# A hybrid decoder block on one core: the input loaded a second time by tokens, its mean squares from row sums on ScalarE, the constants later, and two early output tiles in other PSUM banks

## The chip, the core and the metric

One core of one Trainium2 chip. The metric is the device time of one execution, in microseconds (us), of the kernel as a whole; lower is better. TensorE (PE in the profile) multiplies matrices into PSUM, VectorE (DVE), ScalarE (ACT) and GpSimd (POOL) work element by element, and SyncE (SP) issues the transfers from and to the chip's memory.

## What is computed

One layer of a hybrid block over 1024 tokens of width 1024, all in float32:

```
h = x
proj  = rms_norm(h, norm_mix_g) @ w_in            # 1536 conv columns, 1824 RWKV columns
y     = concat(short_gated_conv(proj[:, :1536]), rwkv7_time_mix(proj[:, 1536:]))
h     = h + y @ w_out
h     = h + square(relu(rms_norm(h, norm_mlp_g) @ w_up)) @ w_down
h     = h + sigmoid(rms_norm(h, norm_ple_g) @ w_ple_gate) * (p @ w_ple_proj)
out   = rms_norm(h, norm_final_g)
rms_norm(h, g) = h * rsqrt(mean(h*h, last axis) + 1e-6) * g
```

The change concerns the first `rms_norm`: the mean of the squares of each token's 1024 input values, and what waits for it.

## The kernel before

**Layout.** The input is held transposed: width on the 128 partitions (8 tiles, called d), tokens along the row, in two halves of 512 tokens (h0, h1). A tile is 128x512. Each product is made of three matmuls so as to keep float32 precision: an operand is split into a high part (`ah`, `wih`, rounded) and the residual (`al`, `wil`), and high x high, low x high and high x low are summed in PSUM.

**The start.** `start()` writes the order of the transfers on SP: the 16 tiles of x with the weights of the first two jobs among them, then the other weights. `load_x` (L434) brings a tile to one of four `tmp` buffers or to one of seven that are still unused (`r`, `k`, `vv`). `split_x` (L443) makes from it `ah` on ScalarE (scaled by the gain) and `al` on VectorE; then it squares the tile on ScalarE and, from the second tile on, adds the square to a running sum in `BK` on GpSimd (L458). A `tmp` buffer is free again when that addition has been done. When the 8 tiles of a half are in, `row_scale` (L465) sums over the partitions with matmuls against a column of ones (L263), takes mean and epsilon (L266, VectorE) and the power -1/2 (L269, GpSimd), spreads the four columns to 128x512 (L272, `tmc`), transposes them on TensorE (L276) and copies the result to `rbc` (L487): the inverse root of each token on all partitions. The norm is thus applied behind the product: each product tile is multiplied by `rbc` when it leaves PSUM (L616).

**The products.** `products()` runs through the jobs, a job being 128 columns of `w_in` (or of `w_out` later), two PSUM tiles (h0 and h1) and 48 matmuls. The first group holds two jobs (96 matmuls), both LoRA inputs; the second is the remaining 32 LoRA columns (32 matmuls, high and residual of the weights side by side in one tile, `wih`); then come r, k and v of the first head pair and so on, with the convolution's jobs in between. I count them as group 0, 1, 2, ... The output tiles come from a ring of three banks, `pmm0` to `pmm2`; only the second job of group 0 takes its two from the four `px` banks, which else serve the recurrence. A bank is free when `shifted` (L590 on) has multiplied its tile by `rbc`. `shifted` runs in the order of the jobs, on ScalarE and VectorE: for each half the product with `rbc`, the token shift, for the 32 columns first the sum of the two halves of the tile (L613), and behind the LoRA inputs tanh and a split.

**The recurrence.** For each of four head pairs and two halves there is a chain of 8 steps (`chain`). A step is three links, each a pair or one of small matmuls into the one bank `pch` and a small instruction on ScalarE or VectorE that reads it: L1044, L1045, then `pe` on ScalarE; L1053, then `uv` on ScalarE; L1065, L1066, then the state `sv` on VectorE (L1072). The matmuls of the jobs are meant to run between the links.

**Order.** All of it is written by strands to a list scheduler (`_Flow`) while the program is built: each strand names an engine, a cost and what it depends on, and the strand that could start first goes next. On the chip each engine runs its instructions in the order so written. A change of a cost or a buffer in one place moves instructions in others.

Of the kernel before, what the change touches and what calls it, by code (L numbers as in the profile page):

```python
# [14 lines left out]
ALU = mybir.AluOpType  # L15
# [197 lines left out]
def block_kernel(ctx: ExitStack, tc: tile.TileContext, a: dict, out: bass.AP):  # L213
# [101 lines left out]
    with tc.manual_schedule():  # L315
# [67 lines left out]
        def flat(t):  # L383
            return t.rearrange("p c t -> p (c t)")
# [58 lines left out]
        def split_x(h, d, xt, rel, hd):  # L443
# [5 lines left out]
            sl = ss[:, h * HT:(h + 1) * HT]  # L449
            ss_n[h] += 1  # L450
            if ss_n[h] == 1:
                e = yield "act", 620, [e]
                nc.scalar.activation(out=sl, in_=xt, func=AF.Square)
            else:
                e = yield "act", 620, [e]
                nc.scalar.activation(out=xt, in_=xt, func=AF.Square)
                e = yield "pool", 1330, [e]
                nc.gpsimd.tensor_tensor(out=sl, in0=sl, in1=xt, op=ALU.add)  # L458
            rel(e)
            ss_n[2 + h] += 1  # L460
            if ss_n[2 + h] == ND:
                fl.spawn(row_scale(h, e))

        def row_scale(h, e):

            ps, dep, rel = yield from fl.take(px, [e])
            e = yield "pe", 750, [e, dep]
            sums_of_squares(ps, ss[:, h * HT:(h + 1) * HT])
            ss_n[4] += 1
            if ss_n[4] == 2:  # L470
                ss_rel(e)
            r = small[:, 4 + 4 * h:8 + 4 * h]
            e = yield "dve", 157, [e]
            mean_plus_eps(r, ps[:, 0:4])
            rel(e)
# [17 lines left out]
        ss, _, ss_rel = BKs()  # L493
        ss = flat(ss)
        ss_n = [0] * 5
# [35 lines left out]
        def start():  # L531
            for g in range(2):
                for h in range(2):
                    for d in range(4):
                        if h == 0 and d < 2:
                            yield from load_w(d, P, g)
                        yield from load_x(h, 4 * g + d)
                if g == 0:
                    e = yield "sp", 700, []
                    nc.sync.dma_start(out=kc, in_=a["cst"])  # L540
                    kc_ready(e)
                    e = yield "sp", 200, []
                    nc.sync.dma_start(out=ident, in_=a["idn"])
                    id_ready(e)
# [6 lines left out]
        def products():  # L551
# [17 lines left out]
            for k, grp in enumerate(groups):  # L569
                out = isinstance(grp[0][0], tuple)  # L570
                halves = grp[0][2]
                for i, (ci, n, _) in enumerate(grp):
                    key = ("o", ci[0]) if out else ci
                    for h in halves:
                        tiles.setdefault(key, {})[h] = pmm() if i == 0 else (yield from fl.take(px))
# [1494 lines left out]
```

## Time and profile before

| | us |
|---|---|
| runs (3) | 1384.71, 1386.5, 1389.36; median 1386.5 |
| the profiled execution's own time | 1384.89 |
| its span in the trace | 1383.0 |
| TensorE busy | 1338.8 (97%) |
| VectorE busy | 918.5 (66%) |
| ScalarE busy | 641.7 (46%) |
| GpSimd busy | 208.0 (15%) |
| granted TensorE clock, mean | 0.984 |

The busy share is over stages with different limits. The trace times each instruction and says for idle time of an engine what ended it. A matmul that is followed at once by the next shows its whole duration, which overlaps the next one's; the pace is the difference of their starts. The granted clock is 1.00 at 2.4 GHz and 0.50 at 1.2 GHz.

### The profile page before, as it was taken

Reading aid. Unit: us, or ns where it says so; the run is one execution under the profiler, and the core shown is the slowest. Engines: PE = TensorE matmul, PEld = TensorE weight load, DVE = VectorE, ACT = ScalarE, POOL = GpSimd, SP = SyncE. Lnnn points to the kernel's source line nnn. Section 1 sums busy time; section 2 is a strip of 40 time slices with the busy share of each in tenths; the row PEclk is TensorE's granted clock in tenths of the full one; section 3 lists DMA queues with packets and bytes.
Section 4 is the critical chain, followed back from the end, with each engine's and each line's share of the span. In section 5 each row is a group of like instructions: output and inputs, shape, how many; then the busy total and the mean of one; then the engine's idle time right before and its main releaser. Section 6 shows DMA issues by size and latency. Waiting matters only on the chain.

```text
span 1383.0 us, 22259 instructions
## 1 busy us (share of the span) xinstructions
PE 1338.8 (97%) x8456; PEld 1097.6 (79%) x8456; DVE 918.5 (66%) x1484; ACT 641.7 (46%) x1210; POOL 208.0 (15%) x409
## 2 busy tenths in 40 slices
PE   8899899999999999998999999999999999999997
PEld 5687688888878787877788888888888888888886
DVE  7756666766866844548876666666556777895455
ACT  6533255354454455434654445545444444654432
POOL 8115314324224320221000000000000000000000
PEclk9999899999999998999999999999999999999999
DMA  5111012111111132653344444435797433443123
GB/s 174 51 59 41 22 28 56 45 29 41 53 36 41 60 113 89 215 183 138 122 165 152 148 160 161 142 116 189 266 352 245 142 108 96 148 133 125 55 69 91
DMA packets 107451, 161.15 MB, mean 117 GB/s; under 512 B 27376, under 2 KB 36848, under 8 KB 107344
## 3 DMA queue, kind: packets, MB, share of 16 engines
q1 hardware_dynamic: 106672, 159.43, 35.8%
q8 instruction: 66, 1.08, 0.3%
q10 hardware_dynamic: 672, 0.30, 0.1%
q14 instruction: 41, 0.34, 0.1%
HBM read 113.56 MB, written 46.14 MB: 115 GB/s over the span
## 4 chain that ended last, share of the span: by engine, by line
PE 88%; DVE 6%; issue 2%; POOL 2%; DMA 1%; ACT 1%; SPq 0%; POOLq 0%; DVEq 0%; ACTq 0%
PE px L1380 23%; PE pmm L563 23%; PE pmm L1380 18%; PE pch L1380 5%; PE px L1943 2%; PE px L1945 2%; PE px L1944 2%; PE px L819 1%; PE pch L1045 1%; PE pch L1066 1%; PE pch L1053 1%; PE pch L1044 1%; PE pch L1065 1%; DVE wil L431 1%; DVE BK L778 1%
## 5 line engine op out<-in xcount | busy, mean ns | idle before, releaser
L563 PE MATMUL pmm<-ah,wih 128*128 128x512 f32 (+1 forms) x544 | 221.9, 409 | 8.2 <-DVE pz L613 4.5
L563 PE MATMUL pmm<-al,wih 128*128 128x512 f32 (+1 forms) x544 | 222.3, 409 | 1.1 <-DVE al L447 1.1
L563 PE MATMUL pmm<-ah,wil 128*128 128x512 f32 x528 | 217.2, 411 | 4.3 <-DVE wil L431 4.3
L1300 ACT CAST ah<-big 128x512 fp32r<-128x512 f32 x176 | 108.5, 621 | 175.9 <-issue 69.5
L1295 DVE TENSOR_TENSOR al<-big,ah 128x512 fp32r<-128x512 f32 x176 | 120.1, 689 | 66.3 <-ACT ah L1300 66.1
L563 PEld LDWEIGHTS pmm<-ah,wih 128*128 128x128 f32 (+1 forms) x544 | 103.4, 190 | 28.6 <-DVE pz L613 4.9
L563 PEld LDWEIGHTS pmm<-al,wih 128*128 128x128 f32 (+1 forms) x544 | 102.8, 189 | 21.7 <-DVE al L447 2.4
L563 PEld LDWEIGHTS pmm<-ah,wil 128*128 128x128 f32 x528 | 101.1, 192 | 22.7 <-DVE wil L431 6.0
L1380 PE MATMUL px<-ah,al 128*128 128x512 f32 x264 | 102.8, 390 | 0.0
L1380 PE MATMUL px<-al,ah 128*128 128x512 f32 x264 | 102.7, 389 | 0.0
L269 POOL TENSOR_TENSOR r<-r,small 128x4 f32<-128x4 f32 x2 | 2.9, 1453 | 663.4 <-DVE r L266 663.4
L1380 PE MATMUL px<-ah 128*128 128x512 f32 x224 | 87.3, 390 | 0.0
L429 ACT CAST wih<-wir 128x512 fp32r<-128x512 f32 (+1 forms) x78 | 47.5, 609 | 83.4 <-PE pmm L563 78.7
L1295 DVE TENSOR_TENSOR al<-A,ah 128x512 fp32r<-128x512 f32 x108 | 73.3, 687 | 18.3 <-ACT ah L1300 18.0
L1380 PE MATMUL pmm<-ah,al 128*128 128x512 f32 x208 | 81.0, 389 | 0.0
L1380 PE MATMUL pmm<-al,ah 128*128 128x512 f32 x208 | 80.9, 389 | 0.0
L1300 ACT CAST ah<-A 128x512 fp32r<-128x512 f32 x108 | 66.7, 618 | 27.0 <-PE pmm L1380 23.3
L431 DVE TENSOR_TENSOR wil<-wir,wih 128x512 fp32r<-128x512 f32 x76 | 57.5, 759 | 31.5 <-ACT wih L429 31.1
L1380 PE MATMUL pmm<-ah 128*128 128x512 f32 x192 | 74.7, 389 | 0.0
L1380 PEld LDWEIGHTS px<-ah,al 128*128 128x128 f32 x264 | 49.6, 188 | 10.5
L1380 PEld LDWEIGHTS px<-al,ah 128*128 128x128 f32 x264 | 49.6, 188 | 10.5
L1072 DVE SCALAR_TENSOR_TENSOR sv<-sv,dct,pch 128x64 f32<-128x64 f32 x60 | 16.8, 279 | 60.3 <-PE pch L1066 60.0
(377 smaller groups left out, 3095.8 us busy)
## 6 DMA issues: line engine op xcount, KB each, us to landing
bd<-h SPq DMA_DIRECT2D x112, 256.0 KB, 2.3
big<-bd SPq DMA_DIRECT2D x112, 256.0 KB, 2.8
big<-in_w_up_dram SPq DMA_DIRECT2D x32, 512.0 KB, 4.1
A<-in_w_down_dram SPq DMA_DIRECT2D x64, 256.0 KB, 4.6
wir<-in_w_in_dram SPq DMA_DIRECT2D x52, 256.0 KB, 2.7
wir<-in_w_out_dram SPq DMA_DIRECT2D x24, 256.0 KB, 3.1
MB<-in_xT_dram SPq DMA_DIRECT2D x16, 256.0 KB, 3.0
hd<-h SPq DMA_DIRECT2D x16, 256.0 KB, 2.1
```

Source lines behind the costliest of these rows:

```text
L429: nc.scalar.copy(ht[:, :, 0:n], rt[:, :, 0:n])
L431: nc.vector.tensor_tensor(out=lt[:, :, 0:n] if n == P else ht[:, :, n:2 * n], in0=rt[:, :, 0:n], in1=ht[:, :, 0:n].bitcast(F32), op=ALU.su ...
L563: nc.tensor.matmul(ps[0:m], wt[:, d, 0:m], xt[:, x, :], start=first and i == 0, stop=end and i == len(ways) - 1)
L778: nc.vector.tensor_tensor(out=BK[q, :, (1 - h) * C:(2 - h) * C], in0=c3(kh)[q], in1=ei[q], op=ALU.mult)
L819: nc.tensor.matmul(g[h][4][:, c, :], BK[hs[h], c0 + c, :], LA[hs[h], c0 + c, 0:3:2, h * C:(h + 1) * C], start=True, stop=True)
L1072: nc.vector.scalar_tensor_tensor(out=nxt, in0=sv[:, c, :], scalar=dct[:, c:c + 1], in1=ps, op0=ALU.mult, op1=ALU.add)
L1295: nc.vector.tensor_tensor(out=out, in0=x, in1=y, op=ALU.subtract)
L1300: nc.scalar.copy(hi, raw)
L1380: nc.tensor.matmul(ps, wt, xt, start=start and i == 0, stop=stop and i == 2, skip_group_check=on)
L1943: nc.tensor.matmul(pg[:, c], r["hi"][:, d, o:o + P], wh[:, c], start=d == 0, stop=False)
L1944: nc.tensor.matmul(pg[:, c], r["lo"][:, d, o:o + P], wh[:, c], start=False, stop=False)
L1945: nc.tensor.matmul(pg[:, c], r["hi"][:, d, o:o + P], wl[:, c], start=False, stop=d == ND - 1)
```

## The change

- The squares, the running sum on GpSimd and the matmuls against ones go out of the first norm. A tile of x is free when `al` has been made.
- `load_tokens()` loads x once more, now as it lies in memory, 128 tokens on the partitions and their 1024 values along the row (512 KB a tile, 8 tiles), into three buffers that are unused so early: the two `MB` and `BK`. Its strand starts behind the 16 tiles of x. From the fourth tile on a load waits for the square of the third tile before it.
- `square_tokens()` squares a tile on ScalarE with `accum_out`, so the row sum falls out as a column of `small`. After four of them `row_scale` goes on as before, from the mean.
- The constants `kc` and the identity are loaded behind the first three token tiles, where they stood between the 8th and the 9th tile of x.
- In `products()`, the h1 tile of group 1 and of group 3 comes from the `px` banks.

```diff
             x_ready[h][d](e)
-            sl = ss[:, h * HT:(h + 1) * HT]
-            ss_n[h] += 1
-            if ss_n[h] == 1:
-                e = yield "act", 620, [e]
-                nc.scalar.activation(out=sl, in_=xt, func=AF.Square)
-            else:
-                e = yield "act", 620, [e]
-                nc.scalar.activation(out=xt, in_=xt, func=AF.Square)
-                e = yield "pool", 1330, [e]
-                nc.gpsimd.tensor_tensor(out=sl, in0=sl, in1=xt, op=ALU.add)
             rel(e)
...
-        def row_scale(h, e):
-
-            ps, dep, rel = yield from fl.take(px, [e])
-            e = yield "pe", 750, [e, dep]
-            sums_of_squares(ps, ss[:, h * HT:(h + 1) * HT])
...
+        def load_tokens():
+
+            places = [g() for g in (MBs, MBs, BKs)]
+            for i in range(NT):
+                t, dep, rel = places[i] if i < 3 else (places[i % 3][0], squared_x[i - 3], None)
+                e = yield "sp", 1500, [dep]
+                nc.sync.dma_start(out=flat(t), in_=a["x"][i * P:(i + 1) * P, :])
+                fl.spawn(square_tokens(i, flat(t), e, places[i % 3][2] if i + 3 >= NT else None))
+
+        def square_tokens(i, t, e, rel):
+            e = yield "act", 1250, [e]
+            nc.scalar.activation(out=t, in_=t, func=AF.Square, accum_out=small[:, 4 + i:5 + i])
+            squared_x[i](e)
+            if rel is not None:
+                rel(e)
+            if i % 4 == 3:
+                fl.spawn(row_scale(i // 4, [*squared_x[i - 3:i], e]))
+
+        def row_scale(h, deps):
+
             r = small[:, 4 + 4 * h:8 + 4 * h]
-            e = yield "dve", 157, [e]
-            mean_plus_eps(r, ps[:, 0:4])
-            rel(e)
+            e = yield "dve", 157, deps
+            mean_plus_eps(r, r)
             e = yield "pool", 900, [e]
             inverse_root(r)
...
-                if g == 0:
-                    e = yield "sp", 700, []
-                    nc.sync.dma_start(out=kc, in_=a["cst"])
-                    kc_ready(e)
-                    e = yield "sp", 200, []
-                    nc.sync.dma_start(out=ident, in_=a["idn"])
-                    id_ready(e)
+            fl.spawn(load_tokens(), 1)
+            e = yield "sp", 200, []
+            nc.sync.dma_start(out=ident, in_=a["idn"])
+            id_ready(e)
+            e = yield "sp", 700, []
+            nc.sync.dma_start(out=kc, in_=a["cst"])
+            kc_ready(e)
...
-                        tiles.setdefault(key, {})[h] = pmm() if i == 0 else (yield from fl.take(px))
+                        tiles.setdefault(key, {})[h] = pmm() if i == 0 and not (h and k in (1, 3)) else (yield from fl.take(px))
```

The order changes in many places. Three of them follow.

On SP, at the end of the x tiles, before (`in_xT` is x transposed, `wir` a weight tile):

```order
L440 DMA tmp_171<-in_xT_dram 128x512
L440 DMA tmp_168<-in_xT_dram 128x512
L418 DMA wir_114<-in_w_in_t_dram 128x4x32
L418 DMA wir_115<-in_w_in_t_dram 128x4x32
L503 DMA tmp_169<-in_w_lora_up_dram 64x512 x2
```

and after:

```order
L440 DMA tmp_168<-in_xT_dram 128x512
L457 DMA MB_120<-in_x_dram 128x1024
L457 DMA MB_121<-in_x_dram 128x1024
L457 DMA BK_181<-in_x_dram 128x1024
L536 DMA ident<-in_idn_dram 128x128
L539 DMA kc<-in_cst_dram 128x279
L457 DMA MB_120<-in_x_dram 128x1024
L457 DMA MB_121<-in_x_dram 128x1024
L457 DMA BK_181<-in_x_dram 128x1024
L418 DMA wir_114<-in_w_in_t_dram 128x4x32
L457 DMA MB_120<-in_x_dram 128x1024
L457 DMA MB_121<-in_x_dram 128x1024
```

The eight token tiles, the identity and the constants now stand between the last tile of x and group 1's weights.

On VectorE, from the mean of the first half to the residual of group 1's weights (`wih` 128x4x32), before:

```order
L266 TENSOR_SCALAR small<-px_108 128x4
L447 SCALAR_TENSOR_TENSOR al_87<-tmp_168,vt,ah_86 128x512
L272 COPY tmc_172<-small 128x512
L519 TENSOR_TENSOR lwl_190<-tmp_169,lwh_188 64x512
L431 TENSOR_TENSOR wih_116<-wir_114,wih_116 128x4x32
L487 COPY rbc<-px_109 128x512
```

and after:

```order
L266 TENSOR_SCALAR small<-small 128x4
L272 COPY tmc_172<-small 128x512
L485 COPY rbc<-px_109 128x512
L612 TENSOR_TENSOR pz_175<-pmm_111,rbc 128x512
L431 TENSOR_TENSOR wih_116<-wir_114,wih_116 128x4x32
L620 SCALAR_TENSOR_TENSOR uv_137<-pz_175,vt,uv_137 128x512
```

The residual that group 1 needs now stands behind `rbc` and the first product with it. On TensorE the transposes of the first half (L276) stood before the last three matmuls of group 0 and now stand right behind them.

On TensorE, in the chain of the second head pair's first half, before (one step, `pmm` rows are matmuls of a job):

```order
L1044 MATMUL pch_110<-va_140,big_77 128x64
L1045 MATMUL pch_110<-sv_142,big_77 128x64
L563 MATMUL pmm_113<-ah_86,wih_116 128x512
L563 MATMUL pmm_113<-al_87,wih_116 128x512
L563 MATMUL pmm_113<-ah_86,wil_118 128x512
L1053 MATMUL pch_110<-pe_152,xi_144 128x64
L563 MATMUL pmm_113<-ah_86,wih_116 128x512
L563 MATMUL pmm_113<-al_87,wih_116 128x512
L563 MATMUL pmm_113<-ah_86,wil_118 128x512
L1065 MATMUL pch_110<-va_140,bt_143 128x64
L1066 MATMUL pch_110<-uv_138,bt_143 128x64
```

and after:

```order
L1040 MATMUL pch_110<-va_140,big_77 128x64
L1041 MATMUL pch_110<-sv_142,big_77 128x64
L1049 MATMUL pch_110<-pe_151,xi_144 128x64
L1061 MATMUL pch_110<-va_140,bt_143 128x64
L1062 MATMUL pch_110<-uv_138,bt_143 128x64
L1040 MATMUL pch_110<-va_140,big_77 128x64
L1041 MATMUL pch_110<-sv_142,big_77 128x64
L1049 MATMUL pch_110<-pe_152,xi_144 128x64
L1061 MATMUL pch_110<-va_140,bt_143 128x64
L1062 MATMUL pch_110<-uv_138,bt_143 128x64
L911 MATMUL px_108<-kc,vv_136 128x128 x4
```

No matmul of a job stands between the links of two steps there.

## Rows read from the trace of the kernel before

**Rows 1.** The page's first line.

```profile
span 1383.0 us, 22259 instructions
```

**Rows 2.** Stretches: sum; PE, PEld, DVE, ACT, POOL busy (instructions); clock; DMA share; GB/s.

```profile
0.00:60.00 60.00, 47.94 (x188) 32.76 (x189) 45.40 (x64) 37.42 (x62) 33.37 (x44) 0.91 0.38 121
```

**Rows 3.** Waits of TensorE, 0 to 140 us: total, times, longest.

```profile
PE pmm L563 <- DVE pz L613: 4.5, 1, 4.5
PE px L962 <- DVE tr L955: 4.2, 1, 4.2
PE pmm L563 <- DVE wil L431: 2.4, 1, 2.4
```

**Rows 4.** Timeline of TensorE: start, duration, instruction, [idle before, what ended it].

```profile
20.19 0.39 PE L563 MATMUL pmm<-al,wih 128*128 128x512 f32 x1
22.97 0.50 PE L563 MATMUL pmm<-ah,wil 128*128 128x512 f32 x1 [2.40 <-DVE wil L431]
...
29.20 1.05 PE L263 MATMUL px<-ones,BK 128*128 128x1 f32 x8
30.11 0.48 PE L563 MATMUL pmm<-ah,wih 128*128 128x512 f32 x1
...
39.00 0.39 PE L563 MATMUL pmm<-ah,wih 128*64 128x512 f32 x1
...
54.22 0.79 PE L563 MATMUL pmm<-ah,wih 128*128 128x512 f32 x1 [4.47 <-DVE pz L613]
...
59.03 0.40 PE L563 MATMUL pmm<-ah,wil 128*128 128x512 f32 x1
...
64.72 0.39 PE L563 MATMUL pmm<-ah,wih 128*128 128x512 f32 x1
```

**Rows 5.** Timeline of VectorE, 0 to 62 us.

```profile
21.16 3.46 DVE L431 TENSOR_TENSOR wil<-wir,wih 128x512 fp32r<-128x512 f32 x2
...
41.20 0.42 DVE L272 COPY tmc<-small 128x512 f32<-128x512 f32 x1
...
44.20 0.69 DVE L487 COPY rbc<-px 128x512 f32<-128x512 f32 x1
...
53.48 0.68 DVE L613 TENSOR_TENSOR pz<-pmm,pz 32x512 f32<-32x512 f32 x1
```

**Rows 6.** Timelines of SP, ACT and POOL, 0 to 62 us: loads, casts, a power.

```profile
12.20 17.30 SPq L440 DMA_DIRECT2D tmp<-in_xT_dram  x5
...
19.02 0.60 ACT L429 CAST wih<-wir 128x512 fp32r<-128x512 f32 x1
...
32.41 0.72 ACT L445 ACTIVATE ah<-tmp,vt 128x512 fp32r<-128x512 f32 x1 [0.36 <-DMA tmp<-in_xT_dram]
...
33.84 1.49 POOL L269 TENSOR_TENSOR small<-small 128x4 f32<-128x4 f32 x1
```

**Rows 7.** Waits of SP's queue, 0 to 40 us.

```profile
SPq L440 <- POOL BK L458: 15.2, 2, 14.4
```

**Rows 8.** Groups of ACT by shape, 1200 to 1383 us: busy, mean ns, idle before.

```profile
L1964 ACT ACTIVATE big<-h 128x512 f32<-128x512 f32 x15 | 9.5, 632 | 20.2 <-DVE h L1963 20.2
L1964 ACT ACTIVATION_READ_ACCUMULATOR big<-h 128x1 f32 x17 | 3.2, 186 | 0.0
L1964 ACT ACTIVATE big<-h 128x256 f32<-128x256 f32 x2 | 0.8, 416 | 3.1 <-DVE h L1963 3.1
```

**Rows 9.** Transfers, 0 to 24 us in 40 slices of 0.6 us.

```profile
GB/s 0 0 17 185 265 390 268 283 341 341 324 328 236 236 300 389 395 387 401 359 270 253 239 358 386 389 372 372 393 181 48 10 0 0 0 0 0 0 0 0
```

**Rows 10.** Stretches of 5 us; the last three rows are of TensorE alone.

```profile
54.00:59.00 5.00, 4.78 (x11) 3.80 (x12) 3.88 (x8) 2.36 (x4) 0.35 (x2) 0.50 0.00 0
...
155.00:160.00 5.00, 3.59 (x22) 0.80 0.13 13
160.00:165.00 5.00, 3.59 (x13) 0.50 0.10 30
165.00:170.00 5.00, 5.00 (x22) 0.68 0.00 0
```

More of the change, by code (lines that the diff above doesn't have):

```diff
@@ L448, in split_x @@
             x_ready[h][d](e)
-            sl = ss[:, h * HT:(h + 1) * HT]
-            ss_n[h] += 1
-            if ss_n[h] == 1:
-                e = yield "act", 620, [e]
-                nc.scalar.activation(out=sl, in_=xt, func=AF.Square)
-            else:
-                e = yield "act", 620, [e]
-                nc.scalar.activation(out=xt, in_=xt, func=AF.Square)
-                e = yield "pool", 1330, [e]
-                nc.gpsimd.tensor_tensor(out=sl, in0=sl, in1=xt, op=ALU.add)
-            rel(e)
-            ss_n[2 + h] += 1
-            if ss_n[2 + h] == ND:
-                fl.spawn(row_scale(h, e))
-        def row_scale(h, e):
-            ps, dep, rel = yield from fl.take(px, [e])
-            e = yield "pe", 750, [e, dep]
-            sums_of_squares(ps, ss[:, h * HT:(h + 1) * HT])
-            ss_n[4] += 1
-            if ss_n[4] == 2:
-                ss_rel(e)
+            rel(e)
+        def load_tokens():
[14 more added lines that the diff above has]
+        def row_scale(h, deps):
             r = small[:, 4 + 4 * h:8 + 4 * h]
-            e = yield "dve", 157, [e]
-            mean_plus_eps(r, ps[:, 0:4])
-            rel(e)
+            e = yield "dve", 157, deps
+            mean_plus_eps(r, r)
             e = yield "pool", 900, [e]
@@ L492, in block_kernel @@
         spare, n_x = [g() for g in (rkv[0], rkv[0], rkv[1], rkv[1], *[vvs] * 3)], [0]
-        ss, _, ss_rel = BKs()
-        ss = flat(ss)
-        ss_n = [0] * 5
+        squared_x = [fl.promise() for _ in range(NT)]
         def lora_weights():
```

## The prediction

> **What bounds the kernel now.** I read the page first, then the busy time by stretches, then TensorE's waits, and then the timelines of the first 65 us engine by engine. The page's span is 1383.0 us [rows 1], and the execution's own time, 1384.89, lies 1.9 above it. TensorE is busy for 97% of the span, so the place to look at is where it is not. The first 60 us are the worst stretch: 47.9 busy of 60, at a mean clock of 0.91 [rows 2]. The waits name what ends the idle time there [rows 3]: 4.5 us for the product at L613, which frees `pmm2`, and 2.4 us for a weight residual. The 4.2 us at L962 belong to the first unit of the recurrence; neither its place in TensorE's order nor the order of VectorE ahead of it changes.
>
> The timeline of TensorE [rows 4] gives three marks. At 20.19 the 50th of group 0's 96 matmuls starts; group 1 starts at 39.00; group 3 starts at 64.72. From 59.03 to 64.72 run 25 matmuls, so the pace at full clock is 0.228 us. Without any wait the 46 matmuls behind 20.42 would end at 30.9, not at 39.0.
>
> Why not: VectorE's two residuals at 21.16 take 3.46 us together, where L613, the same operation, takes 0.68 with GpSimd at rest [rows 5]; GpSimd was adding squares. The 16th tile of x waits 14.4 us in SP's queue for the buffer that GpSimd's addition gives back [rows 7], and ScalarE gets that tile at 32.41 [rows 6]. Matmuls against ones stand in the way: 29.20 to 30.11 for one set, with a second set later. Behind that, group 2 stops at L613, and after 4.47 us of waiting the clock is 0.50 from 54 to 59 [rows 4, 10].
>
> **The change, step by step.**
>
> *Group 0.* The squares and the additions go, so VectorE's residuals should cost 0.69 each again. The first one follows the cast that starts at 19.02 and waits for TensorE, not for data [rows 6]: 19.0 + 0.6 + 0.7 = 20.4 with the hand-over, against a need at 20.4. I allow 0.2 of wait. The 16th tile now needs only the `al` of the 12th. Traffic runs until about 18 us [rows 9], the 12th tile is in three tiles sooner, about 15.8; with 0.72 and 0.75 for its two halves SP issues at 17.4. The old 16th tile was issued at 29.2 and there at 32.4, so 3.2 us [rows 6]: the new one is there at 20.6, long before its matmul. Group 0 then ends at 20.4 + 0.2 + 46 x 0.228 = 31.1, 7.9 us sooner.
>
> *The token tiles.* Each has 512 KB, 1.36 us at the 385 GB/s that the late slices show [rows 9]. Behind the 16th tile the first three land at 22.0, 23.4 and 24.7. No row shows ScalarE with 1024 elements; from 416 ns for 256 and 632 ns for 512 [rows 8] I get 1.06, and 0.19 for reading the sum: 1.25 us. The squares end at 23.3, 24.6, 25.9. The fourth tile waits for the first square, is issued at 23.35 and takes 3.2 + 0.7: there at 27.25, square until 28.5. Mean 0.2, power 1.49 [rows 6], spread 0.42 [rows 5], with hand-overs: `tmc` is ready at 30.9. The transposes stand at 31.1, so TensorE hardly waits for them; the square work hides under group 0.
>
> *A new wait.* Group 1 needs the residual of its weights, which now stands on VectorE behind `rbc` and the first product. Transposes until 31.55, copy 31.8 to 32.5, product to 33.2, residual 0.28: TensorE goes on at 33.6, about 2.1 us idle. Group 1 ends at 33.6 + 32 x 0.228 = 40.9.
>
> *The second half.* Tiles 5 to 8 come round the three buffers the same way; the 8th is there at 33.8. On ScalarE its square stands behind an instruction that reads the first product (33.2): 34.5 to 35.7, the power until 37.5, the spread behind another weight residual at 39.3. The transposes stand two matmuls into group 2, at 41.4, so they do not wait; `rbc` of this half is written from 42.0.
>
> *Groups 2 and 3.* Group 2's h1 tile needs `pmm1`, free at 43.5, wanted at 44.1: no wait. It ends at 40.9 + 0.45 + 48 x 0.228 = 52.3. Group 3 needs `pmm2`. Before, from the second `rbc` copy (44.20) to the end of L613 (54.16) were 9.96 us [rows 5]; the strands between are the same, so 42.0 + 10.0 = 52.0. Just in time. Group 3 starts at 52.3 against 64.72: **12.4 us sooner**. In this are 4.5 of waiting and 2.3 of low clock (11 matmuls from 54.22 to 59.03 at 0.437 instead of 0.228) that go with the second part of the change, the `px` banks. The ends for this step: with no wait behind group 0 the start is at 50.2 (14.5 sooner); at 236 GB/s, the slowest slice in the middle of the flow [rows 9], a tile takes 0.85 more in each of four turns, so 3.4 later (9.0 sooner).
>
> *Clock after the new wait.* After the wait of 2.40 TensorE went on at full pace; after 4.47 it did not [rows 4]. I take the first, which 2.1 is nearest to. The Trainium skill, TensorE: Matmul & The Clock Gate, section on the HAM clock gate, says that the low rate is the default, that activity releases it, and that the moment differs from run to run of one kernel. By that the 2.1 us could also be followed by low clock, and the sum would be 2.3 higher.
>
> *Constants later.* `kc` and the identity (0.2 MB) move behind three token tiles; they are there at about 25.5, and VectorE's first use of `kc` stands ahead of the mean at 28.5. Nothing.
>
> *The recurrence.* Its order up to the second unit is the one of before and follows the products, so it moves along. Behind that, the scheduler has set the job matmuls elsewhere. A chain link with nothing between makes TensorE wait. I counted in both orders: before, 10 of 188 links have nothing between (5 in the first unit, 5 at the end); now 12 (3 in the first unit, 5 in the second pair, 4 at the end). The trace prices them: from 155 to 170 us, where the first five lie, idle is 1.41 + 1.41, and the lower clock costs 3.59 x 0.2 + 3.59 x 0.5 + 5.0 x 0.32 = 4.1 [rows 10], together 6.9, so 1.4 a link. Two more: **+2.8**. The ends: -6.9 (the new stretch is free and the old one gone) and +6.9 (the new one costs as much and nothing comes back).
>
> *The rest* (out projection, MLP, gate) has its instructions in the same order and the same buffers; nothing.
>
> **Sum.** 1384.9 - 12.4 + 2.8 = 1375.3. The median of the runs shown is 1386.5, 1.6 above the profiled one; the likeliest median is about **1376**.
>
> **The rivals.**
>
> *The sums by tokens come late.* Three buffers make a ring of load, square, load; at 236 GB/s, `rbc` is 3.4 later, and since L613 follows 10.0 behind it, group 3 as well; a wait this long may bring the low clock (2.3). 1375.3 + 5.7 = 1381. For it: the margin at `pmm2` is 0.3 us, at the transposes 0.2. Against: late slices run at 385 GB/s. The whole lead is gone only if `rbc` is written after 54, 12 us late. That would be the change not doing what it says.
>
> *The second pair's stretch is harmless.* TensorE may reach it behind its partners, so that the links are ready. Then only the two links that the first unit saves count: 1384.9 - 12.4 - 2.8 = 1369.7. Against: the engines stay in the order in which they were planned.
>
> *The lead is spent in the recurrence.* The jobs run ahead and stop for buffers, and the chain sets the pace. Ten more bare links at 1.4: 1384.9 - 12.4 + 14 = 1386.5. For it: the new stretch itself. Against: fewer bare links at the end.
>
> *Slower: the clock does not come back.* In the second pair's stretch (five bare links) the clock falls to 0.50, and the steps behind it, thin as they are, stay there. Half of each busy microsecond is lost, so beyond 33 us at 0.50 the loss passes 12.4 + 4.2. At 40 us: 1384.9 - 12.4 + 20 = 1392.5. Against: the old stretch was at 0.50 from 160 to 165 us and already at 0.68 in the next five [rows 10].
>
> **How the numbers follow.** A measurement of this kernel can tell about 0.3% from no change, 4.2 us: faster means below 1382.3, slower above 1390.7. Forecast 0.54, tokens late 0.17, harmless stretch 0.13, lead spent 0.10, clock 0.06. Faster: 0.54 + 0.13 and 0.10 of the late tokens, 0.77. Same: the rest of those and the lead spent, 0.17. Slower 0.06. The range takes in the 14.5 and the harmless stretch below, 1367, and the late tokens with a dearer chain above, 1385; beyond it are some 0.04 below and 0.16 above.
>
> **What would show it.** Right: no L263 before the out projection, TensorE's first 128x64 matmul (group 1) at 33 to 34, idle of about 2 us ended by VectorE's `wih` just before it, no wait for L609 (the old L613) over 1 us, group 3 at 52 to 53, VectorE's `al` and `wil` at 0.69 to 0.75. In the recurrence, a new stretch of low clock in the second pair and a shorter one in the first unit. Wrong on the tokens: idle before L276 or a wait for L609. Wrong on the chain: from group 3 on the lead shrinks by more than 7, or grows.

## The result, and the profile after

The changed kernel takes 1372.39 us (median of 6 runs, 1369.56 to 1374.37), the kernel before 1386.77 in the same comparison (6 runs): ratio 0.9892, 95% interval 0.9876 to 0.9909, so 14.4 us less. The forecast was 1376, faster. The profiled execution of the change took 1369.57, 2.8 below its median.

The page's first lines and the row of the first 60 us (sum; PE, PEld, DVE, ACT, POOL busy; clock; DMA share; GB/s), to hold against [rows 1, 2]:

```profile
span 1367.8 us, 22208 instructions
...
PE 1329.6 (97%) x8440; PEld 1089.2 (80%) x8440; DVE 908.4 (66%) x1484; ACT 642.6 (47%) x1210; POOL 188.1 (14%) x395
```

```profile
0.00:60.00 60.00, 54.18 (x223) 39.53 (x224) 37.21 (x67) 39.73 (x64) 12.24 (x31) 0.97 0.60 199
```

TensorE's idle time is the span less its busy time: 44.2 us before (1383.0 - 1338.8), 38.2 now. The time lost to the lower clock is the span times what the mean clock lacks to 1.00: 22.1 before (0.016), 13.7 now (the view of the cores has 0.990). Of the 15.2 us between the two spans 6.0 are idle time and 8.4 are clock; the last digit of the clock is worth 1.4.

In the first 60 us idle time went from 12.1 to 5.8, and the lost clock from 60 x 0.09 = 5.4 to 60 x 0.03 = 1.8. So behind 60 us the idle time is nearly the same, 32.1 and 32.4, and only lost clock differs, 16.7 and 11.9. That split decides most of what follows.

TensorE's waits of the first 140 us in the change (for [rows 3]); L609 is the old L613, L958 the old L962:

```profile
PE px L958 <- DVE tr L951: 3.9, 1, 3.9
PE pmm L559 <- ACT ah L445: 2.3, 2, 1.9
PE pmm L559 <- DVE wih L431: 1.7, 1, 1.7
```

The 4.5 for the sum is gone, as is the 2.4 for a `wil`. In their place stands one wait of 1.7, for the residual of group 1's weights. The timeline of TensorE shows the end of group 0, the start of group 1 and the start of group 3 (for [rows 4]):

```profile
31.93 0.60 PE L276 MATMUL px<-ident,tmc 128*128 128x128 f32 x4
34.24 0.45 PE L559 MATMUL pmm<-ah,wih 128*64 128x512 f32 x1 [1.71 <-DVE wih L431]
...
53.09 0.39 PE L559 MATMUL pmm<-ah,wih 128*128 128x512 f32 x1
```

VectorE's timeline (for [rows 5]), a row of SP's and two of ScalarE's (for [rows 6, 8]):

```profile
20.32 0.69 DVE L431 TENSOR_TENSOR wil<-wir,wih 128x512 fp32r<-128x512 f32 x1 [0.65 <-ACT wih L429]
...
21.68 0.69 DVE L431 TENSOR_TENSOR wil<-wir,wih 128x512 fp32r<-128x512 f32 x1
...
26.85 0.23 DVE L1205 CAST blkr<-kc 128x128 fp32r<-128x128 f32 x1 [3.60 <-DMA kc<-in_cst_dram]
...
29.99 0.17 DVE L266 TENSOR_SCALAR small<-small 128x4 f32<-128x4 f32 x1 [2.78 <-ACT MB L462]
...
33.90 0.28 DVE L431 TENSOR_TENSOR wih<-wir,wih 128x128 fp32r<-128x128 f32 x1
...
42.81 0.69 DVE L485 COPY rbc<-px 128x512 f32<-128x512 f32 x1 [1.54 <-PE px L276]
...
52.05 0.68 DVE L609 TENSOR_TENSOR pz<-pmm,pz 32x512 f32<-32x512 f32 x1
```

```profile
18.35 0.33 SPq L440 DMA_DIRECT2D tmp<-in_xT_dram  x1
```

```profile
23.02 1.06 ACT L462 ACTIVATE MB<-MB 128x1024 f32<-128x1024 f32 x1 [0.55 <-DMA MB<-in_x_dram]
23.98 0.18 ACT L462 ACTIVATION_READ_ACCUMULATOR MB<-MB 128x1 f32 x1
```

Group 3 starts at 53.09 instead of 64.72, 11.6 sooner. From there to the end of the span it took 1383.0 - 64.72 = 1318.3 before and takes 1314.7 now. I call this **the remainder**.

### The profile page after: what moved, and what is told of

Its sections match the earlier page's. It is cut to its first block, busy times and chain, and to the rows that moved or that the text cites. A ratio compares the mean times of both kernels' runs of the same rounds, so it can differ in the third digit from the quotient of the medians.

```text
span 1367.8 us, 22208 instructions
## 1 busy us (share of the span) xinstructions
PE 1329.6 (97%) x8440; PEld 1089.2 (80%) x8440; DVE 908.4 (66%) x1484; ACT 642.6 (47%) x1210; POOL 188.1 (14%) x395
## 4 chain that ended last, share of the span: by engine, by line
PE 89%; DVE 5%; DMA 2%; POOL 2%; issue 1%; ACT 1%; SPq 0%; POOLq 0%; DVEq 0%; ACTq 0%
PE pmm L559 23%; PE px L1376 23%; PE pmm L1376 19%; PE pch L1376 5%; PE px L1939 2%; PE px L1941 2%; PE px L1940 2%; PE px L559 2%; PE px L815 1%; PE pch L1041 1%; PE pch L1062 1%; PE pch L1040 1%; PE pch L1049 1%; PE pch L1061 1%; POOL g L934 1%
## 5 line engine op out<-in xcount | busy, mean ns | idle before, releaser
L559 PE MATMUL pmm<-ah,wih 128*128 128x512 f32 (+1 forms) x528 | 216.7, 410 | 7.9 <-ACT wih L429 2.7
L559 PE MATMUL pmm<-al,wih 128*128 128x512 f32 (+1 forms) x528 | 215.6, 409 | 0.3 <-DVE al L447 0.3
L559 PE MATMUL pmm<-ah,wil 128*128 128x512 f32 x520 | 212.2, 408 | 1.2 <-DVE wil L431 1.2
L559 PEld LDWEIGHTS pmm<-ah,wih 128*128 128x128 f32 (+1 forms) x528 | 100.6, 191 | 27.6 <-ACT ah L445 3.6
L431 DVE TENSOR_TENSOR wil<-wir,wih 128x512 fp32r<-128x512 f32 x76 | 56.6, 746 | 37.3 <-ACT wih L429 36.4
L1044 ACT COPY pe<-pch 128x64 f32<-128x64 f32 x64 | 13.6, 213 | 81.6 <-PE pch L1041 81.5
```

What stands on the lines that cost most here:

```text
L431: nc.vector.tensor_tensor(out=lt[:, :, 0:n] if n == P else ht[:, :, n:2 * n], in0=rt[:, :, 0:n], in1=ht[:, :, 0:n].bitcast(F32), op=ALU.su ...
L559: nc.tensor.matmul(ps[0:m], wt[:, d, 0:m], xt[:, x, :], start=first and i == 0, stop=end and i == len(ways) - 1)
```

## The experiments

The theory: the gain is made in the first 60 us, by the additions that GpSimd no longer makes and by the two banks, and passes one to one into the time. Against it: the prediction's own term for the recurrence (each bare chain link costs 1.4, and the change has two more), and chance in the clock. A bare link is one with no other matmul between the instructions that wait for each other.

All twelve kernels in one table; before and the change stand in it twice, with a second profiled execution each. The median is of the timed runs; group 3, the remainder, idle and lost clock are of the one profiled execution, idle and lost clock of its whole span, worked out as above.

| kernel | median | ratio to before, 95% | group 3 at | remainder | idle | lost clock | bare links |
|---|---|---|---|---|---|---|---|
| before | 1386.8 | | 64.72 | 1318.3 | 44.2 | 22.1 | 10 |
| the change | 1372.4 | 0.9876–0.9909 | 53.09 | 1314.7 | 38.2 | 13.7 | 12 |
| e1 change again | 1368.6 | 0.9865–0.9894 | 51.46 | 1313.8 | 36.8 | 9.6 | 12 |
| e2 banks back | 1381.1 | 0.9956–0.9979 | 61.31 | 1316.4 | 41.8 | 24.8 | 8 |
| e3 banks only | 1389.0 | 1.0015–1.0050 | 57.92 | 1331.7 | 49.1 | 22.2 | 13 |
| e4 constants early | 1375.7 | 0.9916–0.9941 | 54.86 | 1319.0 | 38.7 | 22.0 | 4 |
| e5 no additions | 1373.6 | 0.9899–0.9927 | 56.33 | 1314.9 | 36.7 | 15.1 | 7 |
| e6 square 1350 | 1376.1 | 0.9918–0.9945 | 52.09 | 1322.6 | 40.0 | 20.6 | 13 |
| e7 load 1400 | 1368.5 | 0.9862–0.9895 | 53.47 | 1312.7 | 32.2 | 17.8 | 5 |
| e8 constants 800 | 1375.9 | 0.9913–0.9944 | 51.92 | 1321.7 | 37.7 | 22.0 | 8 |
| e9 residual ahead | 1373.7 | 0.9900–0.9928 | 54.44 | 1319.2 | 36.6 | 24.7 | 12 |
| e10 old order | 1374.5 | 0.9912–0.9944 | 52.81 | 1318.9 | 38.7 | 19.2 | 10 |
| e11 before again | 1385.1 | 0.9987–1.0007 | 65.15 | 1319.8 | 43.2 | 26.3 | 10 |
| e12 new cost | 1362.9 | 0.9824–0.9858 | 52.53 | 1306.8 | 28.6 | 13.6 | 6 |

Before, timed beside e1 to e4, had a median of 1385.6 (21 runs, 1381.07 to 1390.96), beside e5 to e8 1386.0, beside the rest 1385.7.

The profiled execution is not always a middling one. It lies below its kernel's median by 2.8 us in the change, by 1.9 before and by some 1.5 in e1, e2 and e12, and above it by 1.7 in e9 and e11 and by 2.4 in e3; in the others the two agree within 0.6. A difference of two remainders can be off by as much.

**e1, the change once more.** No edit.

> The changed kernel once more, to tell what belongs to the change from what differs between executions. Theory: the gain of the start is fixed, so group 3 starts at 52.2 to 53.0 again and the wait for the residual of group 1's weights is 1.5 to 2.2. What may differ is the stretches of low granted clock: in the profile read so far there is none at the end of the recurrence (515 to 530 us), while before had one of 10 us there; if that was chance, this profile has one, the mean clock is 0.984 to 0.986 and the time 1372 to 1374. Rival: the low stretch at the end went because one bare chain link went, so it is gone again, and the clock is 0.99.

Measured: 1368.56. Group 3 came at 51.46 (the 52.6 that the expectations name was read two matmuls early: it is 53.09). The start is sooner because TensorE's waits for `ah` at the beginning are 0.6 instead of 2.3; the 1.7 for the residual is the same. There is again no low clock at the end of the recurrence, and the mean clock is 0.993: so far the rival. e9, e10 and e11 add three more executions to this (see e11).

**e2, without the banks.**

```diff
-pmm() if i == 0 and not (h and k in (1, 3)) else (yield from fl.take(px))
+pmm() if i == 0 else (yield from fl.take(px))
```

> The change without its last line: the h1 tiles of groups 1 and 3 come from the ring of three banks again. Theory: two waits come back, about 2 us at the start of group 2 (its first tile is the bank that the product with rbc of the second half frees) and 5 to 6.5 at group 2's second tile (the bank that the sum L609 frees at 52 to 53); group 3 then starts at 61 to 63.5 (52.6 with the change), lower figure without a low-clock stretch behind the wait. Bare chain links: 8 instead of 12. Time 1375 to 1383. Rival (the banks matter only with the old, late sums): no wait over 1 us for L609, time within 3 us of 1372.

Measured: group 3 at 61.31, 1381.06. The two waits, from TensorE's waits of 0 to 66 us:

```profile
PE pmm L559 <- DVE pz L609: 4.7, 1, 4.7
...
PE pmm L559 <- DVE pz L612: 1.6, 1, 1.6
```

Behind the longer one the granted clock is 0.50 for 5 us (50 to 55). The time and group 3 are as the theory has it, the two waits a little shorter. The new sums without the banks are worth 3.4 us at group 3; the last line of the diff is worth 8.2 more.

**e3, the banks alone.** In the kernel before:

```diff
-pmm() if i == 0 else (yield from fl.take(px))
+pmm() if i == 0 and not (h and k in (1, 3)) else (yield from fl.take(px))
```

> The kernel before with the last line of the change alone. Theory: the wait of 4.5 for L613 and the low clock behind it (2.3) go, all else of the start stays; group 3 starts at 57.5 to 58.5 (64.7 before). Bare chain links: 13 instead of 10. Time 1379 to 1384. Rival (the wait only moves, to the next tile that waits for a late rbc): group 3 at 62 or later, time 1385 to 1388.

Measured: group 3 at 57.92, 6.8 sooner than before, exactly the 4.5 + 2.3 of the prediction. And the kernel is slower, 1388.96 (ratio 1.0032). The remainder grew by 13.4 us in the profiled executions, and by 10.2 as the medians have it (1389.0 - 1385.6 + 6.8): the planner, given 6.8 us, wrote another order. TensorE's waits from 60 to 600 us there:

```profile
PE px L962 <- DVE tr L955: 6.2, 3, 4.5
PE pmm L563 <- DVE pz L616: 2.8, 2, 1.9
PE pmm L563 <- DVE tmc L1167: 2.5, 1, 2.5
PE px L869 <- DVE lo L864: 2.1, 2, 1.9
```

None of the four is a bare link. The time lies above the ranges of the theory and of its rival: a gain at the start can be lost behind it, and not by links alone.

**e4, the constants early.** In the change, with the same two loads taken away behind the token tiles:

```diff
                         yield from load_x(h, 4 * g + d)
+                if g == 0:
+                    e = yield "sp", 700, []
+                    nc.sync.dma_start(out=kc, in_=a["cst"])
+                    kc_ready(e)
+                    e = yield "sp", 200, []
+                    nc.sync.dma_start(out=ident, in_=a["idn"])
+                    id_ready(e)
             fl.spawn(load_tokens(), 1)
```

> The change with the constants left where they were, between the 8th and the 9th tile of x. The start should not care: group 3 at 51.5 to 53.0. But the scheduler's order of the recurrence comes out otherwise: 4 bare chain links instead of 12. If a bare link costs the 1.4 us of the prediction, the time is 1360 to 1363; if it costs only its idle time (0.4 to 0.8), 1366 to 1369; if the order of the recurrence is worth nothing, or what it saves is lost to other waits, 1371 to 1374.

Measured: 1375.69. With four bare links instead of twelve the remainder is 1319.0, 4.3 longer, and the time lies above all three of the ranges. One price for every link does not fit that. Group 3 came 1.8 later than in the change, at 54.86: TensorE waited 1.6 for `tmc` of the second half and 1.5 for a product behind it. The early constants themselves cost nothing that shows: group 0 ended and group 1 started at 30.48.

**e5, no additions.** In the kernel before:

```diff
                 nc.scalar.activation(out=xt, in_=xt, func=AF.Square)
-                e = yield "pool", 1330, [e]
-                nc.gpsimd.tensor_tensor(out=sl, in0=sl, in1=xt, op=ALU.add)
```

> The kernel before with GpSimd's additions of the squares left out (the mean is then taken of the first tile of each half alone, so the output differs); the squares on ScalarE, the matmuls against ones and the banks stay. Theory: these additions are what holds group 0 up. Without them VectorE's two residuals at 21 us take 0.7 each instead of 3.46 together, the 16th tile of x does not wait for its buffer, and group 1 starts at 31.5 to 33 (39.0 before). The wait for L613 stays at 4 to 5.5 us, since group 2 and the late rbc move together, so group 3 starts at 57 to 58.5 (64.7 before). Behind that the order is that of before up to the second half of the recurrence: time 1377 to 1381. Rival (the late tile is a matter of transfers, and the matmuls against ones hold TensorE): group 1 at 36 or later, time above 1383.

Measured: 1373.59, below the range that I had given. The kernel forms its mean from one tile of eight, so its result is of no use; its time is. VectorE's two residuals and TensorE's wait for the sum (here L611):

```profile
19.29 0.69 DVE L431 TENSOR_TENSOR wil<-wir,wih 128x512 fp32r<-128x512 f32 x1 [1.73 <-ACT wih L429]
20.65 0.69 DVE L431 TENSOR_TENSOR wil<-wir,wih 128x512 fp32r<-128x512 f32 x1 [0.67 <-ACT wih L429]
```

```profile
46.61 0.80 PE L561 MATMUL pmm<-ah,wih 128*128 128x512 f32 x1 [2.64 <-DVE pz L611]
```

Group 1 starts at 33.24 (39.0 before), group 3 at 56.33, 8.4 sooner. The squares on ScalarE and the matmuls against ones are all still there. So it is the additions on GpSimd, and not those, that held group 0 up; the late tile went with them. The wait for the sum shrank by 1.8, which I had not expected: the sum came 7.6 sooner (45.88 against 53.48 in [rows 5]) and group 2 only 5.8 (it starts with the second matmul of the row at 40.82, before of the row at 46.59).

Two things more follow from e5. Leaving out the additions alone takes 12.4 us off the time (1386.0 - 1373.6), most of the change's 14.4 to 17.0. And without the banks group 3 comes 5.0 sooner here (56.33) than in e2 (61.31): `rbc` of the second half is written from 36.64 here, from 41.22 in e2 and from 44.20 before. So the row sums by tokens come 4.6 later than a sum that costs nothing and only 3.0 sooner than the old one, and it is the banks that keep this from holding group 2 up. How e5 would do with the banks was not run.

**e6, e7, e8: one number of the planner.** Each is the change with one cost altered and no instruction more or less.

```diff
-            e = yield "act", 1250, [e]
+            e = yield "act", 1350, [e]
...
-                e = yield "sp", 1500, [dep]
+                e = yield "sp", 1400, [dep]
...
-            e = yield "sp", 700, []
+            e = yield "sp", 800, []
```

> The change with one number of the planner altered: the square of a token tile is entered with 1350 instead of 1250. The instructions are the same and so is their order up to the first head pair's chains; behind that the order of the recurrence comes out otherwise, with 13 bare chain links instead of 12 (3 in the first unit, 5 in the second pair, 5 in a row in the last). Theory 1 (bare links at 1.4 each): 1 to 2 slower than the change, 1370 to 1372 on this chip. Theory 2 (the order of the recurrence is worth several us in either direction, by all its waits and by the low clock behind them, and bare links do not tell which): group 3 within 0.5 of the change's 52.6 or of 51 (the two executions seen), and from there to the first norm of the second half a time that differs by 3 to 10 us from the 561 to 563 of the change.

> The change with another number of the planner altered: the load of a token tile is entered with 1400 instead of 1500. The start's order moves a little (the second transposes one matmul later); the recurrence has 5 bare links, all in the first unit, none later. Theory 1 (1.4 a link): 7 x 1.4 = 9.8 faster than the change, about 1360. Theory 2: as the kernel with 1350, a difference of 3 to 10 us of either sign that the number of bare links does not tell.

> The change with the load of the constants entered with 800 instead of 700. Same order as the change up to the first head pair's chains, then 8 bare links: 3 in the first unit, 5 in the second pair, none at the end. Theory 1: 4 x 1.4 = 5.6 faster than the change, 1363 to 1365. Theory 2: as above, any sign.

Measured: group 3 at 52.09, 53.47 and 51.92, so the start is the change's. The remainders are 1322.6, 1312.7 and 1321.7 against 1314.7 and 1313.8: +8, -1.5, +7.5. The medians agree: by their ratios e6 and e8 are 5 to 7 us slower than the change and e1, with intervals that do not overlap. Theory 1 asked for -10 from e7 and -6 from e8; e8 came out on the other side. e6 and e8 bear theory 2 out, and e7 moved less than the 3 us that it allowed for. Of the two parts, e7 has less idle time than the change's two executions (32.2 against 38.2 and 36.8) and loses as much more to the clock (17.8 against 13.7 and 9.6); e8 has their idle time (37.7) and loses 22.0 to the clock, and e6 is worse in both.

**e9, the residual ahead.**

```diff
+            yield from load_w(-1, 32, 0)
             e = yield "sp", 700, []
             nc.sync.dma_start(out=kc, in_=a["cst"])
             kc_ready(e)
-            for g in range(2):
-                yield from load_w(-1, 32, g)
+            yield from load_w(-1, 32, 1)
```

> The change with one load moved: the first half of group 1's weights is fetched ahead of the constants instead of behind the sixth token tile, so that its residual stands on VectorE ahead of rbc. The order behind the start is that of the change on every engine. Theory: the wait of 1.7 for that residual goes (0.4 or less left); the second transposes stand in TensorE's own order, so rbc and the sum L609 move along and do not become the next wait; group 3 starts 1 to 1.7 sooner than the 52.6 and 50.8 of the two executions seen, and the time is 1366.5 to 1368. Rival (the start is held by the token tiles anyway): a wait of over 1 us for L609 or for the spread, time 1368 to 1370.

**e10, the old order.** In e9:

```diff
-                e = yield "sp", 1500, [dep]
+                e = yield "sp", 1400, [dep]
```

> The kernel of the run with the residual ahead, with the load of a token tile entered in the planner with 1400 instead of 1500. The scheduler then writes the recurrence in the order of before, from group 3 to the end, on TensorE, VectorE and ScalarE; so this is the new start with the old order (10 bare links: 5 in the first unit, 5 at the end). It tells the worth of the start from that of the order. Theory: the start's 12 to 14 us pass through the recurrence one to one, and the order of the change is worth some 3 us more, mostly in low clock: 1370.5 to 1374, 3 to 6 above the run with the residual ahead. Rival, the prediction's own term (the change's order costs 2.8): 1363 to 1365.5, 2.8 below it.

Measured: 1373.67 and 1374.48. e9 is slower than its theory and its rival have it, and group 3 came at 54.44, later than the 53.09 of the change. In both, the wait for group 1's first residual is gone, and TensorE stops in the middle of the group instead, for the second one, whose load still stood behind the last token tile. The wait is the same to the hundredth in both. First e9's row, then e10's; then the stretches 35 to 40 and 40 to 45 us of e9, and of e10 (sum, PE busy, clock, DMA share, GB/s):

```profile
37.79 0.45 PE L559 MATMUL pmm<-ah,wih 128*64 128x512 f32 x1 [2.13 <-DVE wih L431]
```

```profile
37.75 0.44 PE L559 MATMUL pmm<-ah,wih 128*64 128x512 f32 x1 [2.13 <-DVE wih L431]
```

```profile
35.00:40.00 5.00, 2.87 (x10) 0.85 0.79 204
40.00:45.00 5.00, 5.00 (x21) 0.81 0.18 54
```

```profile
35.00:40.00 5.00, 2.87 (x13) 1.00 0.67 187
40.00:45.00 5.00, 5.00 (x26) 1.00 0.17 52
```

The same wait costs 1.7 us of clock in one execution and nothing in the other. As to the orders: from group 3 on e9 has the change's and e10 that of before, and their remainders are 1319.2 and 1318.9. The prediction's term would have made e10 2.8 faster than e9, my theory 3 to 6 slower; it is 0.8 slower, and the intervals overlap. So the two orders are worth the same as far as these runs tell, which is to some 3 us. And the start's gain does pass on: e10 is before with the new start, group 3 comes 11.9 sooner, and the time is 11.2 shorter (1385.7 - 1374.5).

**e11, before once more.** No edit.

> The kernel before once more, to see which of its low-clock stretches belong to its order. Theory: the five links in a row at the end (526 to 531 us) bring the clock to 0.50 again, for 4 us lost or more, since the change without a run of five there had none in two executions; the lost clock behind group 3 is 14 to 20 us (17.0 in the profile read before; 10.4 and 12.3 with the change). Rival (chance): none or a short one there.

Measured: 1385.13. At the end of the recurrence the clock is at 0.50 again, with 1.9 us idle and 0.4 + 2.5 + 0.6 = 3.4 of lost clock, a little less than the 4 of the theory; the first profile of before has the same idle time there and 5.1 lost. Behind 60 us 20.9 are lost, more than the 14 to 20 forecast. The three stretches of e11, then those of e10, whose order is the old one too, and then those of e9 at the same place in the program, where the order is the change's:

```profile
530.00:535.00 5.00, 3.46 (x35) 0.93 0.02 6
535.00:540.00 5.00, 4.64 (x33) 0.50 0.00 0
540.00:545.00 5.00, 5.00 (x29) 0.89 0.43 157
```

```profile
515.00:520.00 5.00, 3.87 (x34) 0.76 0.00 0
520.00:525.00 5.00, 4.64 (x30) 0.50 0.01 3
525.00:530.00 5.00, 5.00 (x23) 0.72 0.47 157
```

```profile
515.00:520.00 5.00, 4.24 (x53) 1.00 0.16 52
520.00:525.00 5.00, 4.22 (x21) 0.82 0.05 18
525.00:530.00 5.00, 5.00 (x18) 0.50 0.44 142
```

The change had 1.5 us of idle time there and kept its clock; so it did in e1. The profile of the change:

```profile
515.00:520.00 5.00, 3.48 (x47) 1.00 0.08 28
520.00:525.00 5.00, 4.99 (x30) 1.00 0.35 114
```

In e9 the same instructions with 1.5 us idle lost 3.4. So at this place the old order, with five bare links in a row, lost 5.1, 3.4 and 5.1 us (before, e11, e10) and the change's, with four, lost 0, 0 and 3.4. The other two places show the same split. In the first unit, behind the links, the old order's five lost 5.1 in each of the three executions (before: [rows 10]), the change's three nothing in any. In the second pair the old order has no bare link and lost nothing; the change's five lost 1.7, 1.7 and 5.1 (the change, e1, e9). The profile of the change there:

```profile
195.00:200.00 5.00, 3.10 (x20) 1.00 0.01 2
200.00:205.00 5.00, 4.21 (x19) 0.66 0.33 82
```

All fourteen profiles together have 17 stretches of five or six bare links within 8 us. At the end of each of them or right behind it the granted clock was at 0.50 for a while (a row gives the mean of its 5 us), in eight for a loss of 5.1 us, in three of 3.4 and in six of 1.7. Of eleven stretches of three or four links, eight lost nothing; the others lost 3.4, 3.4 and 5.1.

So where in the recurrence the clock falls goes with the order, and how much is lost there differs from one execution to the next. Part of what I took for worth of the change's order after e1 was such a difference: behind its links it lost 1.7 in two executions and 8.5 in e9, the old order 10.2, 8.5 and 10.2. This also goes with the spread of the runs of one kernel: of the 21 runs of before beside e1, the one with the mean clock 0.989 took 1381.07 and one with 0.981 took 1390.96.

**e12, a cost set right.** e9, with the planner's cost of one VectorE multiplication (L769 in the trace) at 1500 instead of 690:

```diff
-            e_k = yield "dve", 690, [rk]
+            e_k = yield "dve", 1500, [rk]
             nc.vector.tensor_tensor(out=kh, in0=kh, in1=k, op=ALU.mult)
```

> The run with the residual ahead, and a VectorE multiplication of the preparation (L768) entered with 1500, nearer to the 1.67 us that it takes beside GpSimd, instead of 690. The inverse's operands (L946, L951) then come ahead of the products for BK in VectorE's order, and TensorE's wait of 3.9 for them in the first unit should shrink to 1 to 2.5, with less low clock behind it. The rest of the recurrence is ordered otherwise too (6 bare links, all in the first unit), which by the runs so far may be worth 9 us either way. If the order is no worse than the change's: 1362 to 1366, else up to 1375.

Measured: 1362.87, the fastest of all: ratio 0.9841, the upper end of its interval below the lower ends of the change's two. VectorE ahead of the first unit, in the change run again, and then in e12:

```profile
119.92 1.67 DVE L769 TENSOR_TENSOR tmp<-tmp,k 128x512 f32<-128x512 f32 x1
121.69 3.07 DVE L774 TENSOR_TENSOR BK<-tmp,tmp 64x512 f32<-64x512 f32 x2
124.79 0.69 DVE L946 TENSOR_TENSOR xw<-xc,kc 128x512 f32<-128x512 f32 x1
125.51 0.71 DVE L951 STREAM_TRANSPOSE tr<-xw 128x512 f32<-128x512 f32 x1
```

```profile
121.33 1.67 DVE L769 TENSOR_TENSOR tmp<-tmp,k 128x512 f32<-128x512 f32 x1
122.92 0.68 DVE L946 TENSOR_TENSOR xw<-xc,kc 128x512 f32<-128x512 f32 x1
123.63 0.71 DVE L951 STREAM_TRANSPOSE tr<-xw 128x512 f32<-128x512 f32 x1
...
124.84 1.37 DVE L774 TENSOR_TENSOR BK<-tmp,tmp 64x512 f32<-64x512 f32 x2
```

The transpose for which TensorE waits is made ahead of the pair L774, and the wait, 4.2 in [rows 3] and 3.9 in the change, is 1.0 (TensorE's waits, 60 to 600 us):

```profile
PE px L958 <- DVE tr L951: 1.0, 1, 1.0
```

That accounts for 2.9 of the 8 us of idle time that e12 has less than e9 (28.6 against 36.6). As much again goes with the bare links, 6 instead of 12: the waits for `pe`, `uv` and `sv` between 60 and 600 us are 2.4 instead of 5.2. These and the rest come from the order that the altered cost gave the later units, and whether it would come again with another small edit is open: by e6 to e8 the same kind of edit can give +8.

## Why the prediction was right, point by point

**Group 0: right, 0.8 late.** Forecast to end at 31.1, it ended at 31.93. The residuals take 0.69 each, as forecast. The 16th tile was issued at 18.35 (forecast 17.4) and was never waited for. The 0.8 is a longer wait for `ah` at the beginning, 2.3 in this execution, which e1 did not have.

**The token tiles: right in what they cost, the fourth one late.** The estimate of 1.06 + 0.19 for a square is 1.06 and 0.18 in the trace. The mean of the first half started at 29.99, 1.5 later than forecast (28.5), since the fourth tile's square started at 28.81 and not at 27.25; the power took 1.02 instead of 1.49, and `tmc` was ready at 31.73 (forecast 30.9). The transposes followed the last matmul of group 0 without a wait, 0.2 behind `tmc`.

**The new wait: right.** 2.1 was forecast, for `wih` on VectorE behind `rbc` and the first product; 1.71 it is, and the full clock behind it as well (what the 0.97 of the first 60 us lacks lies before 15 us). That the clock would stay up is the point where I was lucky: with 2.13 it stayed up in e10 and fell in e9. In the prediction I set against it the sentence of the Trainium skill, TensorE: Matmul & The Clock Gate, section on the HAM clock gate, by which the moment differs between runs of one kernel. The trace agrees: before and e11 are one kernel, and at the end of the recurrence they lost 5.1 and 3.4 us; e9 and e10 are two builds, with the same wait.

**Groups 2 and 3: right.** `rbc` of the second half was written from 42.81 (forecast 42.0), L609 ended at 52.73, 9.9 later (forecast 10.0), and group 3 started 0.36 behind it without a wait: just in time, as forecast, at 53.09 instead of 52.3. The gain at this point is 11.6 (13.3 in e1) for the forecast 12.4, inside its ends of 9.0 and 14.5. The 6.8 for the banks is what e3 shows at this place.

**Constants later: nothing, right.** VectorE waited 3.60 for `kc` but went on at 26.85, ahead of the mean at 29.99.

**The recurrence: wrong.** The term "two more: +2.8" failed. The remainder did not grow but shrank, by 3.6 in the profiled pair and by 4.5 with e1; "from group 3 on the lead shrinks by more than 7, or grows" was the prediction's own sign of being wrong on the chain, and the lead grew. The step that failed is the price of 1.4 for every link, wherever it stands. It is made of idle time (2.8 of 6.9 us) and of lost clock (4.1 there, where each stretch was weighted with its busy time; 5.1 by the measure used here) behind five links in a row. The idle part is small: the waits for `pe`, `uv` and `sv` between 60 and 600 us are 5.0 before and 5.2 in the change, a sixth of its 32.4 of idle time.

The clock part came with the stretches, not with the single links. The change has one stretch of five where before has two, and behind its links it lost 1.7, before 10.2: that is 8.5 less. In all only 4.8 less were lost behind 60 us (16.7 and 11.9), since more was lost at other waits. The sign "a new stretch of low clock in the second pair and a shorter one in the first unit" was right; the new one was cheaper than the old ones. With 8.5 lost behind the same links in e9, part of this is chance. No run changes the links alone, so this account is read from the traces and not tested. And the links do not tell the whole: e4 has no stretch of five and lost 22.0 in its span, 5.1 of it at 454 to 465 us where no bare link stands. Over the kernels, 4 links go with a remainder of 1319, 12 with 1314 and (e9) 1319, 8 with 1316 and 1322.

**The sum** was 1375.3 for the profiled execution, which took 1369.57: 0.8 lost at the start, 6.4 won behind it. Both the time and the range held, but not by the term for the recurrence, which had the wrong sign; the range was wide enough for that. The order of the recurrence can move the time by 10 to 13 us up (e3 against before) or 6 to 8 down (e12 against the change), whatever the start gives. That is more than the 6.9 either way that the prediction allowed for it, so it was in part luck that the time stayed in the range. The rival "the lead is spent in the recurrence" had 0.10; e3 is that case, with 6.8 won at the start and 10.2 lost behind it, though by other waits than the ones named. "Harmless stretch", 1369.7, is the nearest of all in number to the 1369.57, but its reason (links that are ready when TensorE comes) is not what the trace shows: in the change's stretch TensorE idles 1.9 + 0.8 = 2.7 us and 1.7 are lost to the clock (the rows of 195 to 205 us).

**What stays open.** The median gained 14.4 and in e1's comparison 17.0, the start 11.6 and 13.3. The mean clock of the timed runs is 0.9845 before (21 runs), 0.986 and 0.9886 for the change (6 and 5 runs): 21.5, 19.2 and 15.6 us lost, of which the start accounts for 3.6. So up to some 2 us of the difference are clock behind the start, and 1 to 3 us have no cause that these runs can name; e10, which has the old order, kept only 11.2. In the mean of many runs a kernel's clock does come again: before has 0.9845, 0.9841 and 0.9846 beside the three groups of experiments and 0.9848 in e11, against 0.9888 in e5 and 0.9900 in e12. What in an order sets this mean is open.

## What to carry to other kernels

In a program whose order a planner writes from costs, forecast the stage that the change touches, and give all behind it a scatter taken from two or three builds that differ by a harmless number: here -1.5 to +8 us, of a gain of 14. Keep idle time and lost clock apart: behind 60 us the idle time of one order came again to within 0.8 us (32.1 and 31.4 for before, 32.4 and 33.0 for the change), while lost clock came again at the stretches of five bare links, but with 1.7 to 5.1 us at each. A price for it needs more than one execution, and its spread belongs in the range. Where a trace shows an instruction at more than twice its planned cost, try the right cost: here that build was the fastest, with 2.9 us from the wait that was aimed at and the rest from an order that may not come again.

## What the runs showed of the hardware

- A VectorE operation with two inputs of 128x512 takes 0.69 us with GpSimd at rest (L431 in the change and in e5). Beside GpSimd's additions two of them took 3.46 together [rows 5]. Beside operations with two inputs on GpSimd (119.5 to 124.2 us in e1), L769 takes 1.67, and the two of L774 (64x512) 3.07 in e1; in e12, where GpSimd rests at that moment, the two take 1.37. Taking GpSimd's work away gave 8.4 us at group 3, though GpSimd itself was busy for only 15% of the span.
- Two waits of 2.13 us at the same instruction were followed by a clock of 0.85 and 0.81 in one kernel and by 1.00 in the other. The same instructions at the end of the recurrence with 1.5 us idle lost 0, 0 and 3.4 us in three executions. At each of 17 stretches of five or six bare links the clock fell to 0.50, for a loss of 1.7 to 5.1 us.
- Squares of 1024 elements with a row sum took 1.06 and 0.18 us on ScalarE, and the second load of the input (4.2 MB more: 165.3 against 161.1 MB in all) cost no wait but the one of 1.7.
